# A causal convolution by matrices: its start rebuilt around an fp32 load of the history rows on SyncE's queue

## The chip, the cores and the metric

One core of a Trainium2 chip (trn2), as the page of the kernel before shows it: TensorE multiplies matrices (3620 matmuls) into tiles that the program keeps in PSUM (`pp` in the views); VectorE and ScalarE work element by element (764 and 460 instructions); loads are issued on GpSimd's queue (64 of x, 8 of the taps, 2 of the history), nearly all stores and the transposes of x on SyncE's (61 transposes); the page's DMA share is a mean over 16 DMA engines. The metric is the device time of one execution in microseconds (us); a run repeats it, and the medians below are of such runs. Experiments were timed on the same chip as the kernel before, in rounds with it. The first comparison was timed in six runs each, beforehand; the changed kernel was not timed again beside the experiments.

## The reference

```python
B, S, D, K = 8, 4096, 512, 8
out = 0
for k in range(K):
    shifted = x shifted down by k rows in S, zeros first      # k = 0: x itself
    out += matmul(shifted, kernel[k])                         # kernel[k] is 512 x 512
```

The sequence is cut into 128 runs of 256 rows, one run per partition (16 runs for each of the 8 batches). A run needs the last rows of the run ahead of it: its **history**. Partition p takes it from partition p-1's rows in memory; partition 0 has none, so a history load has 127 partitions. The first run of each batch (every sixteenth partition) must have zeros there.

## The kernel before

TensorE multiplies in bf16. The eight taps and the rows are combined in three levels of sums and differences (Karatsuba's trick; W holds 8 tap matrices and 19 differences), so that fewer products do. The main loop is steady; what the change touches is the start. There four history rows (H) and the first four rows (`xin[0, 0]`) are transposed and summed on TensorE by multiplying with the identity, `ident`; `identh` is the identity with zeros for the first runs. `direct` is one product of the first sixteen.

```python
def load(out, src):                      # casts fp32 to bf16 on the way
    nc.gpsimd.dma_start(out=out, in_=src)

H = D421
load(H[1:P, 4:8], xr[0:P - 1, RUN - 4:RUN, :])       # history, 127 partitions
load_x(0, 0)
ident = spool.tile([P, P], bf, name="ident")
make_identity(nc, ident)
identh = ...                             # cut: identh, identn, zero, by GpSimd and VectorE

def fill(pw):                            # warm-up: products that nobody reads
    for h in range(2):
        nc.tensor.matmul(pw[:, h], lhsT=ident, rhs=zero, start=True, stop=True)

for r in range(2):
    for k in range(4):
        fill(pair(k))                    # 16 matmuls
...
load_w(4)
transpose_pe("xh", 2, H, 5, 8)
sums_pe("d4a", 1, (-4, 0), (-3, 1))      # history row + x row, transposed, on TensorE
load(H[1:P, 1:4], xr[0:P - 1, RUN - 7:RUN - 4, :])
load_w(6)
sums_pe("d4b", 2, (-2, 2), (-1, 3))
...
direct(0, 2)                             # the first product
```

The first outputs of a node of the main loop go from PSUM into an "ms" buffer, of which there are two, and these also hold finished rows until their stores are done:

```python
mpool = ctx.enter_context(tc.tile_pool(name="m", bufs=2))
...
elif n.a == MID:
    ms[b_] = mpool.tile([P, 2, D], f32, name="ms")
    nc.scalar.copy(out=ms[b_], in_=p)
```

## Time and profile before

| | before |
|---|---|
| median time, 3 runs | 783.0 us (782.42 to 783.3) |
| span of the profiled execution | 780.9 us |
| TensorE busy | 767.4 us, 98% |
| VectorE busy | 659.3 us, 84% |
| history rows landed | 6.9 us |
| first product | 13.81 us |

An engine that is busy 98% of the span leaves only its few idle stretches to win or lose. The view of waits (who waited for whom: us in total, times, longest), cut to the first 100 us, shows those of TensorE after the warm-up; each is about one microsecond:

```profile
PE pp L192 <- DMA xin<-in_x_dram: 1.4, 1, 1.4
...
PE pp L192 <- ACT D L362: 1.1, 1, 1.1
PE pp L192 <- ACT XT L390: 1.1, 1, 1.1
...
PE pp L215 <- DVE pp L76: 0.9, 2, 0.7
PE pp L215 <- DMA w<-in_kernel_dram: 0.9, 1, 0.9
```

### The profile page before, as it was taken

To read this page: it belongs to the slowest core of one execution; us is meant where nothing else is said; L and a number is where in the kernel's file an instruction comes from. 1 tells how busy PE (TensorE), PEld (TensorE's weight loads), DVE (VectorE), ACT (ScalarE), POOL (GpSimd) and SP (SyncE) were. 2 spreads that over 40 slices of the span, in tenths; PEclk is the share of its full clock that TensorE was granted. 3 is DMA by queue.
4 is the path that set the end of the run, shared out by engine and by line. 5 is a ranking of instruction groups with operands and counts; after the bars stand their busy time and mean duration, and the time that the engine had idled before them with its cause. 6 is when DMAs were issued, how large, how long until landed. Compare 5 with 4: busy or idle time off the path is not lost.

```text
span 780.9 us, 9507 instructions
## 1 busy us (share of the span) xinstructions
PE 767.4 (98%) x3620; PEld 349.0 (45%) x3620; DVE 659.3 (84%) x764; ACT 283.2 (36%) x460; POOL 42.8 (5%) x83
## 2 busy tenths in 40 slices
PE   7899999999999999999999999999999999999997
PEld 4444444444444444444444444444444444444443
DVE  4899888888888889888898888898888898888895
ACT  2453433333333333343324343333343333343332
POOL 5000000000000000000000000000000000000000
PEclk9999999999999999999999999999999999999999
DMA  9963979778788777878777788877787877788753
GB/s 163 210 120 114 237 176 207 169 187 167 178 179 206 174 176 173 177 184 194 184 171 168 179 190 188 191 166 179 165 187 187 195 170 182 166 172 200 179 153 123
DMA packets 159229, 138.37 MB, mean 177 GB/s; under 512 B 130130, under 2 KB 134226, under 8 KB 159184
## 3 DMA queue, kind: packets, MB, share of 16 engines
q1 hardware_dynamic: 145312, 98.84, 46.3%
q0 software_dynamic: 13728, 38.66, 31.1%
q8 instruction: 28, 0.46, 0.2%
q10 hardware_dynamic: 144, 0.26, 0.1%
q14 instruction: 17, 0.14, 0.1%
HBM read 77.32 MB, written 67.11 MB: 185 GB/s over the span
## 4 chain that ended last, share of the span: by engine, by line
PE 94%; DMA 3%; DVE 1%; POOL 1%; issue 0%; ACT 0%; DVEq 0%; POOLq 0%
PE pp L215 94%; DMA xin<-in_x_dram 2%; DMA XT<-xin 1%; POOL w L80 0%; DVE D L76 0%; PE pp L192 0%; DVE pp L76 0%; ACT XT L390 0%; DVE y L76 0%; POOL D L80 0%; DVEq L648 0%; POOL xin L80 0%; POOL identn L148 0%; PE pp L186 0%; POOL ident masks.py:199 0%
## 5 line engine op out<-in xcount | busy, mean ns | idle before, releaser
L215 PE MATMUL pp<-w,D 128*128 128x512 bf16 x3280 | 715.8, 379 | 1.7 <-DMA w<-in_kernel_dram 0.9
L215 PEld LDWEIGHTS <-D 128*128 128x128 bf16 x3280 | 320.2, 98 | 390.4 <-issue 2.8
L76 DVE TENSOR_TENSOR D<-D 128x2048 bf16<-128x2048 bf16 (+2 forms) x250 | 227.2, 948 | 3.4 <-ACT D L369 3.4
L76 DVE TENSOR_TENSOR y<-pp,ms 128x1024 f32<-128x1024 f32 (+1 forms) x121 | 146.4, 1212 | 45.3 <-PE pp L215 45.3
L76 DVE TENSOR_TENSOR D<-XT 128x2048 bf16<-128x2048 bf16 (+2 forms) x153 | 142.5, 947 | 12.1 <-DMA XT<-xin 10.4
L262 ACT COPY pp<-pp 128x512 f32<-128x512 f32 x95 | 54.1, 570 | 260.6 <-PE pp L215 260.6
L274 ACT COPY pp<-pp 128x512 f32<-128x512 f32 x95 | 54.2, 570 | 167.1 <-PE pp L215 165.6
L76 DVE TENSOR_TENSOR pp<-dts,pp 128x512 f32<-128x512 f32 x95 | 65.7, 691 | 43.9 <-ACT dts L280 42.6
L317 ACT COPY ms<-pp 128x1024 f32<-128x1024 f32 x60 | 61.0, 1016 | 35.0 <-PE pp L215 33.0
L80 POOL DMA_DIRECT2D xin<-in_x_dram x64 | 34.0, 531 | 692.5 <-DMA XT<-xin 675.8
L290 DVE SCALAR_TENSOR_TENSOR pp<-pp,dts 128x512 f32<-128x512 f32 x95 | 66.0, 695 | 3.2
L280 ACT COPY dts<-pp 128x512 f32<-128x512 f32 x95 | 57.5, 606 | 0.0
L276 ACT ACTIVATE pp<-pp 128x512 f32<-128x512 f32 x95 | 56.1, 590 | 0.8 <-PE pp L215 0.8
L215 PE MATMUL pp<-w,XT 128*128 128x512 bf16 x120 | 30.8, 379 | 0.0
L76 DVE TENSOR_TENSOR w<-w,w 128x2048 bf16<-128x2048 bf16 x19 | 22.9, 1219 | 1.5 <-DMA w<-in_kernel_dram 1.3
L215 PEld LDWEIGHTS <-XT 128*128 128x128 bf16 x120 | 11.7, 98 | 14.2
L186 PE MATMUL pp<-zero,ident 128*128 128x512 bf16 x20 | 6.7, 493 | 3.1 <-POOL ident masks.py:199 3.1
L215 PE MATMUL pp<-w,F 128*128 128x512 bf16 x36 | 8.7, 379 | 0.2 <-DVE pp L76 0.2
L215 PE MATMUL pp<-w,w 128*128 128x512 bf16 x36 | 8.3, 379 | 0.0
L192 PE MATMUL pp<-ident,xin 128*128 128x128 bf16 x48 | 3.2, 219 | 3.6 <-DMA xin<-in_x_dram 1.4
L80 POOL DMA_DIRECT2D w<-in_kernel_dram x8 | 6.1, 785 | 0.5 <-DMA w<-in_kernel_dram 0.5
L358 DVE COPY D<-pp 128x1536 bf16<-128x1536 bf16 x1 | 1.0, 958 | 6.1 <-PE pp L192 6.1
(59 smaller groups left out, 78.7 us busy)
## 6 DMA issues: line engine op xcount, KB each, us to landing
out_dram<-y SPq DMA_DIRECT2D x123, 512.0 KB, 3.4
xin<-in_x_dram POOLq DMA_DIRECT2D x64, 512.0 KB, 6.0
w<-in_kernel_dram POOLq DMA_DIRECT2D x8, 512.0 KB, 15.7
out_dram<-ms SPq DMA_DIRECT2D x2, 512.0 KB, 5.4
out_dram<-f SPq DMA_DIRECT2D x2, 512.0 KB, 6.3
XT<-xin SPq DMA_TRANSPOSE x61, 6.1
D<-in_x_dram POOLq DMA_DIRECT2D x1, 508.0 KB, 5.6
D<-in_x_dram POOLq DMA_DIRECT2D x1, 381.0 KB, 9.4
```

What stands on the lines that cost most here:

```text
L76: nc.vector.tensor_tensor(out=o, in0=a, in1=b, op=op)
L80: nc.gpsimd.dma_start(out=out, in_=src)
L186: nc.tensor.matmul(pw[:, h], lhsT=ident, rhs=zero, start=True, stop=True)
L192: nc.tensor.transpose(o[:, t - t0, c * P:(c + 1) * P], src[:, t, c * P:(c + 1) * P], ident)
L215: nc.tensor.matmul(bank, lhsT=comp[:, c * P:(c + 1) * P], rhs=w[:, c, :], start=start and c == 0, stop=c == DC - 1, skip_group_check=True)
L262: nc.scalar.copy(out=n.q[:, 0], in_=n.q[:, 1])
L274: nc.scalar.copy(out=n.p[b_][:, 1], in_=n.q[:, 1])
L276: nc.scalar.mul(out=n.p[b_][:, 1], in_=n.q[:, 1], mul=-1.0)
L280: nc.scalar.copy(out=n.dts, in_=n.q[:, 0])
L290: nc.vector.scalar_tensor_tensor(out=p[:, 0], in0=p[:, 1], scalar=-1.0, in1=n.dts, op0=MUL, op1=SUB)
L317: nc.scalar.copy(out=ms[b_], in_=p)
L358: nc.vector.tensor_copy(out=XF[:, 0:3], in_=bank["xh"])
```

## The change

The intent: let the history load start first, on a queue of its own, and have GpSimd issue its casting loads before it builds the identity. The load on SyncE's queue does not cast here, so the rows land as fp32 in D421's space, and VectorE and ScalarE cast them. The sums move from TensorE to VectorE, which makes `identh` needless; the warm-up multiplies zeros by zeros, so that it need not wait for the identity, and has 12 matmuls instead of 16. The order of the start after that (some 200 lines) is another one.

```diff
-    H = D421
-    load(H[1:P, 4:8], xr[0:P - 1, RUN - 4:RUN, :])
+    H, HF = XT, D421.bitcast(f32).rearrange("p (t b) d -> p t (b d)", b=2)
+    nc.sync.dma_start(out=HF[1:P], in_=xr[0:P - 1, RUN - 4:RUN, :])
     load_x(0, 0)
-    ident = ...; make_identity(nc, ident); identh = ...; identn = ...
 ...
+    load_w(4)
+    load(H[1:P, 1:4], xr[0:P - 1, RUN - 7:RUN - 4, :])
+    ident = spool.tile([P, P], bf, name="ident")
+    make_identity(nc, ident)
 ...
-            nc.tensor.matmul(pw[:, h], lhsT=ident, rhs=zero, start=True, stop=True)
+            nc.tensor.matmul(pw[:, h], lhsT=zero[:, 0:P], rhs=zero, start=True, stop=True)
 ...
-    for r in range(2):
-        for k in range(4):
-            fill(pair(k))
+    for k in range(6):
+        fill(pair(k % 4))
 ...
-    transpose_pe("xh", 2, H, 5, 8)
-    sums_pe("d4a", 1, (-4, 0), (-3, 1))
+    nc.vector.tensor_copy(out=H[:, 4:6], in_=HF[:, 0:2])
+    nc.scalar.copy(out=H[:, 6:8], in_=HF[:, 2:4])
+    transpose_pe("h0", 3, H, 4, 6)
+    transpose_pe("h1", 0, H, 6, 8)
+    nc.scalar.copy(out=XF[:, 0:2], in_=bank["h0"])
+    transpose_pe("x0", 2, xin[0, 0], 0, 2)
+    nc.scalar.copy(out=XF[:, 4:6], in_=bank["x0"])
+    tt(D4[:, 0:2], XF[:, 0:2], XF[:, 4:6], ADD)          # the first sum, on VectorE
 ...                                                       (the rest is order)
```

More of the change, by code (lines that the diff above doesn't have):

```diff
@@ L136, in pair @@
         return ppool.tile([P, 2, D], f32, name=f"pp{k}")
-    H = D421
-    load(H[1:P, 4:8], xr[0:P - 1, RUN - 4:RUN, :])
+    H, HF = XT, D421.bitcast(f32).rearrange("p (t b) d -> p t (b d)", b=2)
+    nc.sync.dma_start(out=HF[1:P], in_=xr[0:P - 1, RUN - 4:RUN, :])
     load_x(0, 0)
-    ident = spool.tile([P, P], bf, name="ident")
-    make_identity(nc, ident)
-    identh = spool.tile([P, P], bf, name="identh")
-    nc.gpsimd.tensor_copy(out=identh, in_=ident)
-    nc.gpsimd.memset(identh[:, 0:P:G], 0.0)
-    identn = spool.tile([P, P], bf, name="identn")
-    nc.gpsimd.tensor_scalar_mul(out=identn, in0=ident, scalar1=-1.0)
     zero = spool.tile([P, D], bf, name="zero")
@@ L151 @@
     U1 = zero
-    nc.vector.memset(H[0:1], 0.0)
+    nc.vector.memset(HF[0:1], 0.0)
+    nc.vector.memset(H[0:1, 1:4], 0.0)
     def load_w(tap):
@@ L168, in mid_dve @@
         tt(o, u, v, SUB)
+    load_w(4)
+    load(H[1:P, 1:4], xr[0:P - 1, RUN - 7:RUN - 4, :])
+    ident = spool.tile([P, P], bf, name="ident")
+    make_identity(nc, ident)
     bank = {}
-    def mid_pe(h, k, *which):
-        o, u, v = mid(*which)
-        bank[which, h] = pair(k)
-        for c in range(2):
-            pw = bank[which, h][:, c]
-            nc.tensor.matmul(pw, lhsT=ident, rhs=u[:, 2 * h + c], start=True, stop=False)
-            nc.tensor.matmul(pw, lhsT=identn, rhs=v[:, 2 * h + c], start=False, stop=True)
-    def mid_act(h, *which):
-        nc.scalar.copy(out=mid(*which)[0][:, 2 * h:2 * h + 2], in_=bank[which, h])
     def fill(pw):
         for h in range(2):
-            nc.tensor.matmul(pw[:, h], lhsT=ident, rhs=zero, start=True, stop=True)
+            nc.tensor.matmul(pw[:, h], lhsT=zero[:, 0:P], rhs=zero, start=True, stop=True)
     def transpose_pe(name, k, src, t0, t1):
@@ L194, in transpose_pe @@
         bank[name] = o[:, 0:t1 - t0]
-    def sums_pe(name, k, *sums):
-        pw = bank[name] = pair(k)
-        for h, ts_ in enumerate(sums):
-            for c in range(DC):
-                for n, t in enumerate(ts_):
-                    src, idt = (xin[0, 0][:, t], ident) if t >= 0 else (H[:, 8 + t], identh)
-                    nc.tensor.matmul(pw[:, h, c * P:(c + 1) * P], lhsT=src[:, c * P:(c + 1) * P],
-                                     rhs=idt, start=n == 0, stop=n == len(ts_) - 1,
-                                     skip_group_check=True)
-    for r in range(2):
-        for k in range(4):
-            fill(pair(k))
+    for k in range(6):
+        fill(pair(k % 4))
     XF = D42
@@ L346, with first_run @@
     C0, C1 = W[MID, HI, MID], W[MID, LO, MID]
-    load_w(4)
-    transpose_pe("xh", 2, H, 5, 8)
-    sums_pe("d4a", 1, (-4, 0), (-3, 1))
-    load(H[1:P, 1:4], xr[0:P - 1, RUN - 7:RUN - 4, :])
-    load_w(6)
-    sums_pe("d4b", 2, (-2, 2), (-1, 3))
-    nc.vector.tensor_copy(out=XF[:, 0:3], in_=bank["xh"])
-    transpose_pe("xf", 2, xin[0, 0], 0, 4)
-    load_w(5)
-    nc.vector.tensor_copy(out=D4[:, 0:2], in_=bank["d4a"])
-    nc.scalar.copy(out=D4[:, 2:4], in_=bank["d4b"])
-    n0.p = {0: pair(0), 1: pair(1)}
+    def first_run(z):
+        nc.vector.memset(z[:, :, 0:D:G], 0.0)
@@ new lines @@
+    nc.vector.tensor_copy(out=H[:, 4:6], in_=HF[:, 0:2])
+    nc.scalar.copy(out=H[:, 6:8], in_=HF[:, 2:4])
+    n0.p = {0: pair(0), 1: pair(1)}
+    load_w(6)
+    transpose_pe("h0", 3, H, 4, 6)
+    transpose_pe("h1", 0, H, 6, 8)
+    nc.scalar.copy(out=XF[:, 0:2], in_=bank["h0"])
+    first_run(XF[:, 0:2])
+    transpose_pe("x0", 2, xin[0, 0], 0, 2)
+    nc.scalar.copy(out=XF[:, 4:6], in_=bank["x0"])
+    tt(D4[:, 0:2], XF[:, 0:2], XF[:, 4:6], ADD)
+    load_w(5)
+    transpose_pe("xb", 3, xin[0, 0], 2, 4)
@@ L364 @@
+    nc.scalar.copy(out=XF[:, 2:4], in_=bank["h1"])
+    direct(0, 0)
+    nc.vector.tensor_copy(out=XF[:, 6:8], in_=bank["xb"])
+    first_run(XF[:, 2:4])
     fill(pair(3))
+    transpose_pe("he", 1, H, 1, 4)
+    tt(D4[:, 2:4], XF[:, 2:4], XF[:, 6:8], ADD)
     load_w(7)
+    load_x(0, 1)
+    tt(D2, XF[:, 1:6], XF[:, 3:8], ADD)
     direct(0, 2)
+    direct(0, 3)
+    load_x(1, 0)
+    tt(E4[:, 1:4], bank["he"], XF[:, 1:4], ADD)
+    direct(2, 2)
     direct(0, 1)
-    direct(0, 3)
-    nc.scalar.copy(out=XF[:, 3:7], in_=bank["xf"])
@@ L370 @@
-    sums_pe("e4a", 2, (-5, -1), (-6, -2))
-    nc.vector.memset(XF[:, 0:3, 0:D:G], 0.0)
-    tt(D2, XF[:, 0:5], XF[:, 2:7], ADD)
-    direct(2, 3)
-    tt(F21, D2[:, 0:4], D2[:, 1:5], ADD)
-    mid_dve(1, LO, HI)
-    sums_pe("e4b", 2, (-7, -3))
-    direct(1, 2)
-    direct(0, 0)
-    load_x(0, 1)
-    tt(D1, XF[:, 2:4], XF[:, 3:5], ADD)
-    mid_dve(2, LO, HI)
-    nc.scalar.copy(out=E4[:, 3:1:-1], in_=bank["e4a"])
-    mid_dve(2, LO, LO)
-    load_x(1, 0)
-    load_w(0)
-    nc.vector.tensor_copy(out=E4[:, 1], in_=bank["e4b"][:, 0])
@@ L387 @@
-    direct(1, 3)
-    direct(1, 1)
-    transpose_pe("x1", 2, xin[0, 1], 0, 4)
-    nc.scalar.copy(out=XT[:, 4:8], in_=bank["x1"])
+    first_run(E4[:, 1:4])
+    direct(1, 1)
+    tt(D1, XF[:, 3:5], XF[:, 4:6], ADD)
+    mid_dve(1, LO, HI)
+    nc.vector.tensor_copy(out=F0, in_=XF[:, 4])
+    mid_dve(2, LO, HI)
+    tt(F21, D2[:, 0:4], D2[:, 1:5], ADD)
+    direct(2, 0)
+    mid_dve(2, LO, LO)
     load_w(2)
     mid_dve(1, LO, LO)
+    load_w(0)
+    direct(1, 3)
+    direct(2, 3)
+    mid_dve(2, LO, MID)
@@ L393 @@
     direct(1, 0)
-    transpose_pe("x2", 2, xin[1, 0], 0, 4)
-    mid_dve(2, LO, MID)
-    load_w(1)
-    tt(D4[:, 4:8], XF[:, 3:7], XT[:, 4:8], ADD)
-    direct(2, 1)
-    nc.vector.tensor_copy(out=XT[:, 2:4], in_=bank["x2"][:, 2:4])
+    transpose_pe("x1", 2, xin[0, 1], 0, 4)
+    nc.vector.tensor_copy(out=XT[:, 4:8], in_=bank["x1"])
+    tt(D4[:, 4:8], XF[:, 4:8], XT[:, 4:8], ADD)
+    direct(1, 2)
+    tt(D42[:, 3], D4[:, 1], D4[:, 3], ADD)
+    transpose_pe("x2", 2, xin[1, 0], 0, 4)
+    prep_d41(HI)
@@ L400 @@
+    direct(3, 2)
+    nc.scalar.copy(out=XT[:, 0:2], in_=bank["x2"][:, 0:2])
+    direct(3, 3)
+    nc.scalar.copy(out=XT[:, 2:4], in_=bank["x2"][:, 2:4])
+    nc.scalar.copy(out=C0[:, 0:2], in_=XT[:, 6:8])
+    nc.scalar.copy(out=C1, in_=XT[:, 0:4])
     prep_d42(HI)
-    nc.scalar.copy(out=XT[:, 0:2], in_=bank["x2"][:, 0:2])
-    nc.scalar.copy(out=C0[:, 0:2], in_=XT[:, 6:8])
     tt(T4, XT[:, 4:8], XT[:, 0:4], ADD)
+    direct(3, 0)
+    fill(pair(2))
     direct(3, 1)
-    prep_d41(HI)
-    tt(T42[:, 0:2], D4[:, 6:8], T4[:, 0:2], ADD)
@@ L407 @@
-    direct(3, 0)
-    nc.scalar.copy(out=C1, in_=XT[:, 0:4])
-    direct(2, 0)
-    nc.scalar.copy(out=F0, in_=XF[:, 3])
-    direct(3, 3)
-    fill(pair(2))
     tt(D41[:, 1], T4[:, 0], T4[:, 1], ADD)
     load_w(3)
+    node_a1(1)
+    direct(2, 1)
+    node_u(nodes[1])
+    tt(D41[:, 0], D4[:, 7], T4[:, 0], ADD)
+    tt(T42[:, 0:2], D4[:, 6:8], T4[:, 0:2], ADD)
+    tt(D421[:, 0], D42[:, 7], T42[:, 0], ADD)
     tt(T42[:, 2:4], T4[:, 0:2], T4[:, 2:4], ADD)
-    node_a1(1)
-    direct(2, 2)
+    mid_dve(1, HI, HI)
@@ L418 @@
+    load_w(1)
     node_e(nodes[0], 0)
-    tt(D41[:, 0], D4[:, 7], T4[:, 0], ADD)
+    load_x(1, 1)
+    load_x(2, 0)
+    prep_d27()
+    mid_dve(2, HI, LO)
     node_a0(nodes[1])
-    node_u(nodes[1])
-    direct(3, 2)
-    mid_dve(1, HI, HI)
     node_seed(nodes[1], 0)
-    prep_d27()
+    node_v(nodes[1], 0)
     node_dts(nodes[1])
+    tt(D421[:, 1:4], T42[:, 0:3], T42[:, 1:4], ADD)
+    node_d(nodes[1], 0)
     node_seed(nodes[1], 1)
-    tt(D42[:, 3], D4[:, 1], D4[:, 3], ADD)
-    node_v(nodes[1], 0)
@@ L430 @@
-    tt(D421[:, 0], D42[:, 7], T42[:, 0], ADD)
-    load_x(1, 1)
+    mid_dve(1, HI, LO)
+    node_e(nodes[0], 1)
+    mid_dve(2, HI, HI)
     node_v(nodes[1], 1)
-    tt(D421[:, 1:4], T42[:, 0:3], T42[:, 1:4], ADD)
+    mid_dve(2, HI, MID)
+    node_l(nodes[1], 0, HI)
+    load_x(2, 1)
+    node_d(nodes[1], 1)
+    prep_d421(HI)
+    mid_dve(0, HI, HI)
     node_a1(2)
-    mid_dve(2, HI, LO)
+    node_l(nodes[1], 0, LO)
+    node_e(nodes[1], 0)
     transpose_x(1, 1)
-    mid_dve(1, HI, LO)
-    node_d(nodes[1], 0)
@@ L439 @@
-    node_l(nodes[1], 0, LO)
-    mid_dve(2, HI, MID)
-    nc.scalar.copy(out=D4[:, 2:4], in_=T4[:, 2:4])
-    node_d(nodes[1], 1)
-    load_x(2, 1)
-    node_e(nodes[0], 1)
-    node_u(nodes[2])
-    node_l(nodes[1], 0, HI)
-    node_e(nodes[1], 0)
-    node_a0(nodes[2])
-    node_seed(nodes[2], 0)
-    prep_d421(HI)
-    load_x(2, 0)
-    mid_dve(2, HI, HI)
-    node_l(nodes[1], 1, LO)
-    node_l(nodes[1], 1, HI)
-    nc.scalar.copy(out=U1, in_=XT[:, 0])
-    node_v(nodes[2], 0)
-    prep_d4(HI)
@@ L458 @@
-    nc.scalar.copy(out=D42[:, 3], in_=T42[:, 3])
-    node_seed(nodes[2], 1)
-    node_v(nodes[2], 1)
-    node_dts(nodes[2])
-    mid_dve(0, HI, HI)
-    node_e(nodes[1], 1)
-    prep_d41(HI)
-    node_d(nodes[2], 0)
-    node_l(nodes[2], 0, HI)
-    tt(A1[:, 0], C0[:, 1], C1[:, 0], ADD)
-    prep_d42(HI)
-    node_d(nodes[2], 1)
-    transpose_x(2, 0)
-    mid_dve(0, LO, HI)
+    node_a0(nodes[2])
+    node_u(nodes[2])
+    node_l(nodes[1], 1, LO)
+    node_seed(nodes[2], 0)
+    prep_d4(HI)
@@ L472 @@
+    nc.scalar.copy(out=D4[:, 2:4], in_=T4[:, 2:4])
+    node_l(nodes[1], 1, HI)
+    node_seed(nodes[2], 1)
+    node_dts(nodes[2])
+    node_v(nodes[2], 0)
+    node_d(nodes[2], 0)
+    node_e(nodes[1], 1)
+    node_v(nodes[2], 1)
+    node_l(nodes[2], 0, HI)
+    nc.scalar.copy(out=D42[:, 3], in_=T42[:, 3])
+    prep_d41(HI)
+    mid_dve(0, LO, LO)
+    nc.scalar.copy(out=U1, in_=XT[:, 0])
     node_a1(3)
     node_l(nodes[2], 0, LO)
+    node_d(nodes[2], 1)
     node_a0(nodes[3])
     node_e(nodes[2], 0)
-    mid_dve(0, LO, LO)
+    prep_d42(HI)
@@ L477 @@
+    node_l(nodes[2], 1, LO)
+    node_u(nodes[3])
+    node_seed(nodes[3], 0)
+    node_l(nodes[2], 1, HI)
+    mid_dve(0, HI, LO)
+    node_seed(nodes[3], 1)
     tt(D421[:, 0:4], D42[:, 3:7], D42[:, 4:8], ADD)
-    node_u(nodes[3])
-    node_l(nodes[2], 1, HI)
-    node_seed(nodes[3], 1)
-    node_seed(nodes[3], 0)
+    node_e(nodes[2], 1)
     node_dts(nodes[3])
+    mid_dve(0, LO, HI)
+    node_v(nodes[3], 1)
+    tt(A1[:, 0], C0[:, 1], C1[:, 0], ADD)
     mid_dve(1, MID, HI)
-    node_v(nodes[3], 1)
+    node_v(nodes[3], 0)
@@ L485 @@
     node_d(nodes[3], 1)
-    mid_dve(0, HI, LO)
-    node_v(nodes[3], 0)
     node_d(nodes[3], 0)
-    node_l(nodes[2], 1, LO)
     node_a1(4)
+    node_l(nodes[3], 1, HI)
     mid_dve(1, MID, LO)
+    node_l(nodes[3], 0, LO)
+    node_a0(nodes[4])
+    node_l(nodes[3], 0, HI)
+    node_dts(nodes[4])
     tt(D21[:, 2:4], C1[:, 0:2], C1[:, 2:4], ADD)
-    node_l(nodes[3], 1, HI)
-    node_l(nodes[3], 0, LO)
     mid_dve(2, MID, MID)
-    node_e(nodes[2], 1)
+    tt(D21[:, 0:2], C0[:, 0:2], C1[:, 0:2], ADD)
@@ L497 @@
+    tt(A1[:, 1], C1[:, 0], C1[:, 1], ADD)
     load_x(3, 0)
-    node_l(nodes[3], 0, HI)
-    node_a0(nodes[4])
-    tt(D21[:, 0:2], C0[:, 0:2], C1[:, 0:2], ADD)
+    transpose_x(2, 0)
+    mid_dve(2, MID, LO)
+    node_e(nodes[3], 0)
     node_u(nodes[4])
-    node_e(nodes[3], 0)
+    node_seed(nodes[4], 0)
+    mid_dve(2, MID, HI)
     node_l(nodes[3], 1, LO)
-    tt(A1[:, 1], C1[:, 0], C1[:, 1], ADD)
-    mid_dve(2, MID, LO)
-    mid_dve(2, MID, HI)
-    node_seed(nodes[4], 0)
+    node_seed(nodes[4], 1)
@@ L508 @@
     node_v(nodes[4], 0)
-    node_seed(nodes[4], 1)
-    node_dts(nodes[4])
+    node_e(nodes[3], 1)
     node_d(nodes[4], 0)
@@ L513 @@
     node_v(nodes[4], 1)
-    prep_m()
     node_l(nodes[4], 0, HI)
     node_l(nodes[4], 0, LO)
+    node_u(nodes[5])
+    prep_m()
     node_a0(nodes[5])
-    node_e(nodes[3], 1)
+    node_seed(nodes[5], 0)
     node_d(nodes[4], 1)
-    node_u(nodes[5])
-    node_seed(nodes[5], 0)
+    node_y(nodes[4], 0, LO)
+    tt(F21[:, 0], D2[:, 0], D21[:, 0], ADD)
+    node_y(nodes[4], 0, HI)
     node_l(nodes[4], 1, LO)
-    tt(F21[:, 0], D2[:, 0], D21[:, 0], ADD)
+    prep_d4(LO)
     node_l(nodes[4], 1, HI)
-    node_y(nodes[4], 0, LO)
-    node_y(nodes[4], 0, HI)
-    store(0, LO, 0, first[0, LO, 0])
-    tt(F21[:, 1], D21[:, 0], D21[:, 1], ADD)
     node_dts(nodes[5])
     node_v(nodes[5], 0)
+    store(0, LO, 0, first[0, LO, 0])
+    node_seed(nodes[5], 1)
+    node_y(nodes[4], 1, LO)
     prep_d27()
-    node_seed(nodes[5], 1)
+    node_d(nodes[5], 0)
+    node_v(nodes[5], 1)
+    node_d(nodes[5], 1)
     store(0, HI, 0, first[0, HI, 0])
+    tt(F21[:, 1], D21[:, 0], D21[:, 1], ADD)
+    node_y(nodes[4], 1, HI)
+    node_a1(6)
+    node_l(nodes[5], 0, LO)
+    node_a0(nodes[6])
     load_x(3, 1)
-    node_y(nodes[4], 1, LO)
-    node_v(nodes[5], 1)
-    node_d(nodes[5], 0)
-    node_d(nodes[5], 1)
+    transpose_x(2, 1)
+    node_l(nodes[5], 0, HI)
+    store(0, LO, 1, first[0, LO, 1])
+    node_u(nodes[6])
     tt(F21[:, 2:4], D21[:, 1:3], D21[:, 2:4], ADD)
-    node_l(nodes[5], 0, LO)
-    node_l(nodes[5], 0, HI)
-    node_a1(6)
-    node_l(nodes[5], 1, HI)
-    node_u(nodes[6])
-    prep_d4(LO)
-    store(0, LO, 1, first[0, LO, 1])
-    node_y(nodes[4], 1, HI)
-    node_a0(nodes[6])
-    node_y(nodes[5], 0, LO)
-    prep_d41(LO)
-    transpose_x(2, 1)
-    node_l(nodes[5], 1, LO)
-    store(0, HI, 1, first[0, HI, 1])
-    node_seed(nodes[6], 0)
-    node_v(nodes[6], 0)
-    node_y(nodes[5], 0, HI)
+    prep_d41(LO)
+    node_y(nodes[5], 0, HI)
+    node_l(nodes[5], 1, LO)
+    node_seed(nodes[6], 0)
+    store(0, HI, 1, first[0, HI, 1])
+    node_y(nodes[5], 0, LO)
+    node_v(nodes[6], 0)
+    node_l(nodes[5], 1, HI)
+    store(1, LO, 0, first[1, LO, 0])
+    node_dts(nodes[6])
+    store(1, HI, 0, first[1, HI, 0])
     tt(D21[:, 0:2], D2[:, 0:2], D2[:, 1:3], ADD)
-    node_dts(nodes[6])
+    node_d(nodes[6], 0)
+    node_y(nodes[5], 1, HI)
+    node_y(nodes[5], 1, LO)
     node_seed(nodes[6], 1)
@@ L561 @@
     tt(D21[:, 2:4], D2[:, 2:4], D2[:, 3:5], ADD)
-    node_d(nodes[6], 0)
+    node_d(nodes[6], 1)
     prep_d42(LO)
-    node_y(nodes[5], 1, HI)
-    node_d(nodes[6], 1)
-    store(1, LO, 0, first[1, LO, 0])
-    node_y(nodes[5], 1, LO)
-    store(1, HI, 0, first[1, HI, 0])
+    store(1, HI, 1, first[1, HI, 1])
     node_a1(7)
-    store(1, HI, 1, first[1, HI, 1])
     prep_d4(HI)
```

## The prediction

> **What bounds the kernel now.** I read the page first (the shares of the engines, then the same in 40 slices), then the windows view for the start, then the timeline and the landings of the first loads. The page says which engine is the limit:
>
> ```profile
> PE 767.4 (98%) x3620; PEld 349.0 (45%) x3620; DVE 659.3 (84%) x764; ACT 283.2 (36%) x460; POOL 42.8 (5%) x83
> ...
> PE   7899999999999999999999999999999999999997
> ...
> L215 PE MATMUL pp<-w,D 128*128 128x512 bf16 x3280 | 715.8, 379 | 1.7 <-DMA w<-in_kernel_dram 0.9
> ```
>
> TensorE is busy in 98% of the span, and its products waited 1.7 us in all. So only the start and the tail can change the time. The windows view (columns: stretch and length; busy of PE, PEld, DVE, ACT, POOL with counts; clock; DMA share; GB/s) splits the span where the first product starts (13.8):
>
> ```profile
> 0.00:13.80 13.80, 9.51 (x78) 5.67 (x79) 4.36 (x5) 2.52 (x3) 6.97 (x17) 1.00 0.85 147
> 13.80:34.00 20.20, 16.57 (x116) 8.76 (x115) 15.78 (x17) 8.57 (x7) 4.62 (x7) 1.00 1.19 207
> 34.00:100.00 66.00, 64.99 (x297) 28.71 (x296) 62.83 (x76) 29.53 (x47) 2.11 (x4) 1.00 0.70 159
> 100.00:700.00 600.00, 600.00 (x2781) 271.48 (x2779) 511.40 (x594) 216.28 (x361) 27.48 (x52) 1.00 0.79 181
> ```
>
> TensorE lacks 3.6 us in 13.8 to 34, 1.0 in 34 to 100, nothing in 100 to 700. Before 13.8 it does only warm-up, transposes and sums. Its whole time is therefore: 13.8 us to the first product, then 767.1 us of nearly closed work up to 780.9. In the start the DMA engines are full (share 1.19, 207 GB/s from 13.8 to 34). The timeline (start, length, engine, line, operation, wait before) shows the four rows of history first in the queue, the warm-up and the first products:
>
> ```profile
> 1.23 0.68 POOL L80 DMA_DIRECT2D D<-in_x_dram  x1 [0.80 <-POOLq L637]
> ...
> 3.10 5.51 PE L186 MATMUL pp<-zero,ident 128*128 128x512 bf16 x16 [3.10 <-POOL ident masks.py:199]
> ...
> 13.81 2.75 PE L215 MATMUL pp<-w,D 128*128 128x512 bf16 x12
> ```
>
> and the page's DMA issues (KB each as written, median us from issue to landing) give its duration:
>
> ```profile
> D<-in_x_dram POOLq DMA_DIRECT2D x1, 508.0 KB, 5.6
> ```
>
> The history load (127 partitions of 4 rows, 508 KB as written in bf16) takes 5.6 us from issue to landing, so it is there at 6.9, before the 16 warm-up matmuls end.
>
> [...] (5.6 us for a 127-partition load cannot be one engine, see below). No run so far has a 127-partition load on SyncE's queue; its stores have 128 partitions.
> [...] warm-up matmuls start 0.43 us apart from 3.1 to 6.9, later ones run at about 0.216 us.
>
> **The change part by part.**
>
> *History load on SyncE's queue.* The rate of one DMA engine: software-queue loads move 38.66 MB by the page, while HBM was read for 77.32 MB, so a casting load reads twice what the GB/s column counts. 207 GB/s written over 16 engines is 207 x 2 / 16 = 26 GB/s read for each engine. Stores fit: a 512 KB store, 1.3 us at that rate, lands 3.4 us after issue, so some 2 us are fixed. The load now reads 127 x 8192 B = 1.04 MB. On all engines that is 2.5 us; on one it is 1.04 MB / 26 GB/s = **40 us**. That engine also has its sixteenth of the casting loads queued meanwhile: x rows, four taps, three history rows, x rows; 6.75 loads of 1 MB, at 2.5 us each (1.05 MB / (26 x 16) GB/s), so 17 us. If both queues are served in turn, the casting loads end first and the history needs 40 + 17 = 57 us of this engine; if the short packets of the taps (2 KB read) get less of it, some 52. With 2 us to the first packet and the receipt, I choose landing at **58.5 us**, instead of 6.9.
>
> *After the landing.* The casts of the rows (VectorE two, ScalarE two) come first in their engines' order, and TensorE's first transposes wait for them, so nothing useful passes by. Chain: cast of 128x1024, 1.0 (ScalarE's 128x1024 copies take 1.01 to 1.05); [...] ScalarE's copy of them 1.0 and of the x transposes 1.0; VectorE's sum of 128x1024, 0.7; hand-overs 0.3: 5.2 us. First product at 58.5 + 5.2 = 63.7.
>
> *After the first product.* The same products follow, 767.1 us before. The waits of the old start for DMA mostly go: 3.6 us lacking in 13.8 to 34, as the four taps and two blocks of x have landed by then. The next x block is issued when the x transposes have freed its buffer (4.6 us after the landing) and needs 5.1 as a lone load does here at 45.6; the last four taps follow 2.5 us apart, up to 20 us after the landing, ahead of the node that needs them (22 products of 0.86 us after the first). After the first product 44 small transposes at 0.055 us stand in place of 56 transposes and sums: 0.7 less. [...] VectorE is busy 62.8 of 66 us in 34 to 100 and gets about 3.5 us more work (two sums, a longer E4 sum, larger copies, two clearings): I put half of it, 1.7, on the path. Sum: 767.1 - 3.6 - 0.7 + 1.0 + 1.7 = 765.5.
>
> *The rest.* Identity later and its two variants gone: GpSimd's, off the path. Warm-up on zeros: starts at about 1.1 instead of 3.1, four matmuls fewer; worth nothing if the data come at 58. The steady state and tail are unchanged.
>
> Span 63.7 + 765.5 = 829.2; the reported time lies 2.1 above the span (783.0 against 780.9): **831 us**, 6.1% longer.
>
> **Rivals.**
> (a) *The load is spread over 16 engines.* For it: the author's intent, and that GpSimd's 127-partition load is spread. Then it lands near 7 to 8 us beside the x rows, the chain of 5.2 gives a first product at about 12, some 2 us earlier; but the 12.75 MB of the start still need 12.75 x 2.5 = 32 us of full DMA, so later waits move little: 778 to 785, same. [...]
> (b) *One engine, but with a greater share or faster.* If SyncE's queue is served first, landing near 44 to 49: 816 to 822. Served last or with slower 8 KB rows: up to 65, 838.
> (c) *VectorE becomes the limit of the start.* All of its first 60 us of work now follows the landing, with no idle to work ahead (it had 3.4 and 1.3 us waits before). If all its added 3.5 us and some order conflicts count: 834 to 838. If (a) holds, it makes 785 to 788 and eats the gain.
>
> **Range and chances.** One engine: I give it 88%; (a) has 12%. Within one engine the landing has the spread 48 to 63, and the rest plus or minus 3. Time 831, range 817 to 840. The 2% border is at 798.7: slower 0.87; same 0.12; faster 0.01.
>
> **What would show it.** The page's DMA issues: the history load on SP with 45 to 60 us to landing (about 5 to 7 would be rival a). The 40 slices: TensorE empty from about 6 to near 60. The chain that ended last: some 7% on the DMA of the history rows. The DMA share falls to about a sixteenth between the end of the queued loads and the landing. TensorE's first product within 4 to 7 us of the landing and nearly no gaps after 70. The prediction is wrong if the load is spread, if TensorE finds other work ahead of it, or if VectorE's waits after the landing add up to over 5 us.

With them went the ground for one engine, so that the 88% stand as the author's estimate, and two terms of the sums: 1.2 us for eight transposes, in a chain that came to 5.2 us, and 1.0 us for a restart of TensorE at half clock, in a sum after the first product that came to 767.1 - 3.6 - 0.7 + 1.0 + 1.7 = 765.5. The 63.7, 829.2 and 831 us contain both. What was measured of them stands below, under "Why the prediction was right".

## The result, and the profile after

| | before | after |
|---|---|---|
| median time, 6 runs each | 783.28 us | 835.73 us (835.38 to 837.62) |
| span of the profiled execution | 780.9 us | 833.5 us |
| history rows landed | 6.9 us | 56.95 us |
| first product | 13.81 us | 63.25 us |
| first product to end | 767.1 us | 770.25 us |

The ratio is 1.0677 (95% interval 1.0663 to 1.069). Ratios here are the mean time of one kernel's fast runs over that of the other's of the same rounds, so not quite the ratio of the medians quoted.

The page of the changed kernel, in its parts: engines, the 40 slices, and the DMA issues (KB, us to landing).

```profile
PE 768.4 (92%) x3576; PEld 348.5 (42%) x3576; DVE 661.6 (79%) x770; ACT 281.8 (34%) x460; POOL 41.2 (5%) x79
...
PE   2018998999999999999999999999999999999997
...
DMA  9009448677787778887777787787778778778753
...
D<-in_x_dram SPq DMA_DIRECT2D x1, 1016.0 KB
```

TensorE does the same work (768.4 against 767.4 us) in a longer span: the second and third slice, 21 to 62 us, are empty or nearly so. The DMA engines are nearly empty then too: something is slow, but the memory is not busy. The issue row gives no landing for the history load (nor do those of e2_two); it is read from who waited for it. The waits of the first 125 us:

```profile
ACT L333 <- DMA D<-in_x_dram: 57.0, 1, 57.0
DVE XT L332 <- DMA D<-in_x_dram: 52.9, 1, 52.9
...
PE pp L180 <- DVE XT L332: 51.2, 1, 51.2
```

Two engines wait for one transfer, and TensorE waits for one of them. The windows view says how fast that transfer ran (last two columns: DMA share and GB/s):

```profile
4.00:20.00 16.00, 2.50 (x6) 0.60 (x4) 0.07 (x1) 0.00 (x0) 2.54 (x4) 0.70 1.16 209
22.00:56.00 34.00, 0.00 (x0) 0.00 (x0) 0.00 (x0) 0.00 (x0) 0.00 (x0) 0.50 0.07 23
```

A DMA share of 0.07 is one engine of sixteen (0.0625) and a little more; 23 GB/s is a ninth of what the sixteen write at 4 to 20. The timeline from the landing to the first product:

```profile
56.95 1.28 ACT L333 ACT_TABLE_LOAD   x1 [56.95 <-DMA D<-in_x_dram]
56.98 0.69 DVE L332 CAST XT<-D 128x1024 bf16<-128x1024 f32 x1 [52.91 <-DMA D<-in_x_dram]
...
58.25 1.04 ACT L333 CAST XT<-D 128x1024 bf16<-128x1024 f32 x1
59.20 1.00 ACT L338 COPY D<-pp 128x1024 bf16<-128x1024 bf16 x1
...
61.27 1.01 ACT L341 COPY D<-pp 128x1024 bf16<-128x1024 bf16 x1 [1.07 <-PE pp L180]
...
63.25 1.02 PE L191 MATMUL pp<-w,D 128*128 128x512 bf16 x4 [1.29 <-ACT D L345]
```

It is the chain that was foreseen, with one link more: ScalarE's first instruction is now behind the wait, and its table load of 1.28 us with it. In the kernel before that load ran at 0.72 us, where it cost nothing.

One loss stands far from the start. The timeline at 125 to 137 us:

```profile
125.46 0.53 POOL L80 DMA_DIRECT2D xin<-in_x_dram  x1 [21.96 <-DMA XT<-xin]
...
126.77 0.33 SPq L276 DMA_DIRECT2D out_dram<-ms  x1
...
134.82 1.01 ACT L293 COPY ms<-pp 128x1024 f32<-128x1024 f32 x1 [4.87 <-DMA out_dram<-ms]
...
136.38 1.06 PE L191 MATMUL pp<-w,D 128*128 128x512 bf16 x3 [2.77 <-ACT pp L250]
```

ScalarE waited 4.87 us for a store of an ms buffer to be done, and TensorE 2.77 us for ScalarE. The store took some 8 us from issue (126.77); the kernel before has the same store at 77.96, ahead of its x load, and no such wait of TensorE:

```profile
77.96 0.44 SPq L300 DMA_DIRECT2D out_dram<-ms  x1
...
79.78 0.53 POOL L80 DMA_DIRECT2D xin<-in_x_dram  x1 [23.66 <-DMA XT<-xin]
```

The experiments come back to this order. In the windows 136 to 138 and 138 to 140 the granted clock (TensorE's speed as a share of the full one) is 0.70 and 0.50: the pause also cost TensorE its clock for a while.

### The profile page after: what moved, and what is told of

Its sections match the earlier page's. It is cut to its first block, busy times and chain, and to the rows that moved or that the text cites. A ratio compares the mean times of both kernels' runs of the same rounds, so it can differ in the third digit from the quotient of the medians.

```text
span 833.5 us, 9433 instructions
## 1 busy us (share of the span) xinstructions
PE 768.4 (92%) x3576; PEld 348.5 (42%) x3576; DVE 661.6 (79%) x770; ACT 281.8 (34%) x460; POOL 41.2 (5%) x79
## 3 DMA queue, kind: packets, MB, share of 16 engines
q0 software_dynamic: 13584, 38.14, 29.4%
HBM read 77.32 MB, written 67.11 MB: 173 GB/s over the span
## 4 chain that ended last, share of the span: by engine, by line
PE 82%; DVE 7%; another core or an unknown queue 7%; DMA 2%; issue 1%; ACT 1%; DVEq 0%; SPq 0%; ACTq 0%
PE pp L191 82%; DVE D L76 3%; DVE w L76 2%; DVE y L76 1%; DMA out_dram<-ms 1%; DMA XT<-xin 1%; DVE pp L266 0%; DVE pp L76 0%; PE pp L180 0%; ACT pp L250 0%; ACT L333 0%; DVE F L76 0%; DVE XT L378 0%; DVE ms L76 0%
## 5 line engine op out<-in xcount | busy, mean ns | idle before, releaser
L76 DVE TENSOR_TENSOR D<-D 128x1024 bf16<-128x1024 bf16 (+1 forms) x252 | 228.4, 946 | 1.9 <-ACT D L341 1.7
L76 DVE TENSOR_TENSOR y<-pp,ms 128x1024 f32<-128x1024 f32 (+1 forms) x121 | 146.5, 1211 | 47.2 <-PE pp L191 47.2
L293 ACT COPY ms<-pp 128x1024 f32<-128x1024 f32 x60 | 61.0, 1016 | 36.8 <-PE pp L191 31.9
L180 PE MATMUL pp<-ident,XT 128*128 128x128 bf16 x28 | 2.9, 271 | 51.8 <-DVE XT L332 51.2
L180 PEld LDWEIGHTS <-XT 128*128 128x128 bf16 x28 | 2.3, 122 | 53.2 <-DVE XT L332 52.1
L191 PEld LDWEIGHTS <-XT 128*128 128x128 bf16 x120 | 11.7, 98 | 14.2
```

The lines of the kernel that those rows point to most:

```text
L76: nc.vector.tensor_tensor(out=o, in0=a, in1=b, op=op)
L180: nc.tensor.transpose(o[:, t - t0, c * P:(c + 1) * P], src[:, t, c * P:(c + 1) * P], ident)
L191: nc.tensor.matmul(bank, lhsT=comp[:, c * P:(c + 1) * P], rhs=w[:, c, :], start=start and c == 0, stop=c == DC - 1, skip_group_check=True)
```

## The experiments

Two theories stood at the beginning. **One engine**: SyncE's queue puts a load of 127 partitions on one DMA engine, so 1.04 MB take 50 us instead of 3. **The rest of the change**: fp32 rows, casts on chip, sums on VectorE and the new order cost the time, or fp32 rows 512 KB apart are slow to read whoever asks. Eleven kernels were run, all correct; the times of the kernel before beside them are 783.6 us.

| run | edit on | median us | ratio to before (95%) | history landed | first product |
|---|---|---|---|---|---|
| e1_spread | after | 788.56 | 1.0059 (1.0046 to 1.0072) | 7.6 | 13.86 |
| e2_two | after | 811.15 | 1.0351 (1.0332 to 1.037) | 32.5 | |
| e3_gpsimd | after | 789.05 | 1.0063 (1.0049 to 1.0076) | 8.6 | |
| e4_before_sync | before | 833.65 | 1.0638 (1.0619 to 1.0657) | 57 | 67.70 |
| e5_act | after | 836.40 | 1.0674 (1.0661 to 1.0688) | 57.0 | 62.51 |
| e6_ms | after | 831.64 | 1.0613 (1.0599 to 1.0627) | 57 | |
| e7_spread_ms | after | 782.67 | 0.9991 (0.9979 to 1.0003) | 7.5 | 13.72 |
| e10_spread_warm | after | 781.16 | 0.9977 (0.9964 to 0.999) | 7.3 | 12.78 |
| e11_all | after | 780.87 | 0.9965 (0.9952 to 0.9977) | 7.4 | 11.94 |
| e12_rows | after | 843.28 | 1.0761 (1.0739 to 1.0783) | 63.1 | 69.36 |
| e13_act_warm | after | 834.24 | 1.0648 (1.0632 to 1.0665) | 57 | 61.40 |

### e1_spread: the same load, same queue, in two parts

```diff
-    nc.sync.dma_start(out=HF[1:P], in_=xr[0:P - 1, RUN - 4:RUN, :])
+    nc.sync.dma_start(out=HF[1:113], in_=xr[0:112, RUN - 4:RUN, :])
+    nc.sync.dma_start(out=HF[113:P], in_=xr[112:P - 1, RUN - 4:RUN, :])
```

> The changed kernel with the history load cut in two on the same SyncE queue: 112 partitions [...] and 15 partitions. Theory (the 127-row load sits on one DMA engine): both parts land within 10 us of the start instead of 56.9, first product at 11 to 14 us, time 781 to 791 (835.7 less some 49 us of later landing, with DMA waits of the start coming back). Rival (the reordered start, the fp32 buffer and the casts on chip cost the time): stays over 820.

Measured: 788.56 us. Both parts landed by 7.6 us; the page's DMA issues:

```profile
D<-in_x_dram SPq DMA_DIRECT2D x1, 896.0 KB, 6.0
...
D<-in_x_dram SPq DMA_DIRECT2D x1, 120.0 KB, 6.3
```

How many engines each part had was not read; 896 KB in 6.0 us are 153 GB/s, by an estimate six engines' worth or so at the 26 GB/s of one (e12_rows below). Two lines in place of one take 47.2 of the 52.4 us away. The bytes, the queue, the fp32 buffer and the casts are what they were, so none of those is the main cost. The remaining 5 us, with a first product at 13.86 as early as before (13.81), are a second question.

### e2_two: a dose between

122 and 5 partitions, in the expectation that the larger part is spread over two engines.

```diff
-    nc.sync.dma_start(out=HF[1:P], in_=xr[0:P - 1, RUN - 4:RUN, :])
+    nc.sync.dma_start(out=HF[1:123], in_=xr[0:122, RUN - 4:RUN, :])
+    nc.sync.dma_start(out=HF[123:P], in_=xr[122:P - 1, RUN - 4:RUN, :])
```

> The changed kernel with the load cut into 122 partitions [...] and 5. Theory: 61 rows per engine at the 0.43 us per row that the changed kernel showed (54.9 us for 127), so landing at about 29 us and a time of about 808 (803 to 813), half way between one engine and sixteen. Rival (a fixed cost of this queue or of casts): 835 or, if cutting in two alone helps, as with 112 and 15.

Measured: 811.15 us, landing at 32.5. The share of busy DMA engines while only this load runs doubles, and so does its rate:

```profile
24.00:31.00 7.00, 0.00 (x0) 0.00 (x0) 0.00 (x0) 0.00 (x0) 0.00 (x0) 0.50 0.13 43
```

0.13 is two of sixteen engines (0.125). The landing was 3.5 us later than expected, the time within the expected range. Landing at 7.6, 32.5 and 57 us gives 788.6, 811.2 and 835.7: from 32.5 to 57 the time follows one for one, and below that nearly so. Nothing useful goes past this transfer.

### e3_gpsimd: the same fp32 load, issued by GpSimd

```diff
-    nc.sync.dma_start(out=HF[1:P], in_=xr[0:P - 1, RUN - 4:RUN, :])
+    nc.gpsimd.dma_start(out=HF[1:P], in_=xr[0:P - 1, RUN - 4:RUN, :])
```

> The changed kernel with the same fp32 load of 127 partitions issued by GpSimd instead of SyncE, nothing else changed. Theory (the queue's way of spreading 127 partitions): lands within 10 us, time 781 to 791. Rival (fp32 rows of 8 KB at a pitch of 512 KB are slow to read on any queue): over 820.

Measured: 789.05 us, with 7.4 us from issue to landing, in one piece with all 127 partitions. So fp32 rows of 8 KB, 512 KB apart, are read about as fast as e1_spread's two parts (6.0 and 6.3 us); it is the queue that makes the difference for 127 partitions: 7.4 us here, and a landing at 56.95 on SyncE's. A queue of its own was not worth much: 0.5 us separates this run from e1_spread, less than their spread.

### e4_before_sync: this part alone, in the kernel before

```diff
-    load(H[1:P, 4:8], xr[0:P - 1, RUN - 4:RUN, :])
+    HF = XT.bitcast(f32).rearrange("p (t b) d -> p t (b d)", b=2)
+    nc.sync.dma_start(out=HF[1:P], in_=xr[0:P - 1, RUN - 4:RUN, :])
 ...
+    nc.vector.tensor_copy(out=H[:, 4:6], in_=HF[:, 0:2])
+    nc.scalar.copy(out=H[:, 6:8], in_=HF[:, 2:4])
```

> The kernel before with this one part of the change alone: the four history rows loaded as fp32 on SyncE's queue into the idle XT buffer and cast by VectorE and ScalarE; order, sums and warm-up as before. Theory: landing at about 57 us, time 822 to 835. Rival (the reordered start is what costs): 783 to 787.

Measured: 833.65 us. The old order with this one load is within 2.1 us of the whole change. Together with e1_spread and e3_gpsimd the main question is settled: it is the load, both when taken out and when put in alone.

### e12_rows: who gets how much of the shared engine

The prediction had the casting loads end first, as both queues would be served in turn. In the changed kernel they did not: the first tap landed at 25.8, the last casting load at 61.8, five us after the history. In the trace the history's packets are 8192 bytes, the taps' packets 1024 bytes as written, so 2 KB as read (the page has 38.14 MB written by the casting loads' queue, and HBM read for 77.32 MB). Four loads of one row each make the history's packets 2 KB too.

```diff
-    nc.sync.dma_start(out=HF[1:P], in_=xr[0:P - 1, RUN - 4:RUN, :])
+    for t in range(4):
+        nc.sync.dma_start(out=HF[1:P, t], in_=xr[0:P - 1, RUN - 4 + t, :])
```

> The changed kernel with the history load issued as four loads of one row each: still 127 partitions, one engine, but packets of 2 KB instead of 8 KB. Theory (an engine serves its two queues one packet each in turn): the taps' packets read 2 KB too, so the taps get half of the engine instead of a fifth; the first tap lands near 16 instead of 25.8, all casting loads by 42 instead of 61.8, and the history last, near 60; time 836 to 840. Rival (shares are by time or bytes, whatever the packets): first tap still near 25, history near 57, 835.7. Counter-result for the one-engine theory: landing under 30.

Measured: the first tap landed at 15.5 us (13.6 after its issue, against 23.9 in the changed kernel), the last casting load at 37.9 and the history at 63.1. The view of the first tap in the changed kernel, then in this one:

```profile
DMA to landing us min/median/max: 23.9/23.9/23.9
...
DMA to landing us min/median/max: 13.6/13.6/13.6
```

That fits packets taken turn and turn about. The list of packets in the trace of the changed kernel shows it directly: from 22 to 56 us exactly one packet of the casting loads lies between any two of the history's (83 times of 83); with a tap's packet such a pair takes about 0.4 us, 0.32 of it the history's, so about four fifths. The time, 843.28 us, was above the expected 836 to 840, as the history landed 3 us later than I had reckoned. The reckoning was too low: the engine shared by both queues was done with them at 61.8 us in the changed kernel already. While the history has its engine alone (39 to 59 us of this run) the rate is 26 GB/s, so it is not the short packets that are slow. The landing and the time move together, by 6.1 and 7.6 us against the changed kernel. The other 1.5 us were not followed up; in this run's profile TensorE was at half clock until about 78 us, nine us past the first product, and in the changed kernel's it was not.

### e6_ms: the stall at 134 us

```diff
-            ms[b_] = mpool.tile([P, 2, D], f32, name="ms")
+            ms[b_] = (F21.bitcast(f32).rearrange("p (t b) d -> p t (b d)", b=2)
+                      if n.k == 6 and b_ == LO else mpool.tile([P, 2, D], f32, name="ms"))
```

> The changed kernel, with the first output buffer of the first node of the main loop taken from F21 (idle by then) instead of a buffer whose store is still under way. Theory: the wait of ScalarE of 4.87 us for that store cost TensorE 2.77 us of idle time and then some 1.7 us at half clock, so the time falls by 3.5 to 5, to about 831. Rival: TensorE would be held there by something else (VectorE, the next store) and the time stays within 1 us of 835.7.

Measured: 831.64 us, 4.1 less. ScalarE's copy no longer waits for a store, and TensorE runs through. Timeline of this kernel:

```profile
127.48 12.89 PE L191 MATMUL pp<-w,D 128*128 128x512 bf16 x59
...
131.13 1.01 ACT L294 COPY F<-pp 128x1024 f32<-128x1024 f32 x1 [1.10 <-PE pp L191]
```

### e5_act: the table load off the path

```diff
+    warm = spool.tile([1, 16], bf, name="warm")
+    nc.scalar.copy(out=warm, in_=zero[0:1, 0:16])
     nc.vector.tensor_copy(out=H[:, 4:6], in_=HF[:, 0:2])
```

> The changed kernel with a tiny ScalarE copy first, so that its table load (1.28 us, now behind the wait for the history rows) is done while they are still on their way. Theory: on the path from landing to first product, which shortens by 0.8 to 1.3, time about 834.6. Rival: VectorE's cast sets the first transposes and the table load is hidden: no change. Nearly the size of the noise; the trace (landing to first product, 6.3 us so far) decides.

Measured: 836.40 us, no gain, though the first product came at 62.51 instead of 63.25. In its profile the clock was at 0.50 from 57 to 64, and the first products ran at half speed; in the profile of the changed kernel it was at full speed from 62 on (the changed kernel, then this one; the clock is the column before the last two):

```profile
62.00:64.00 2.00, 0.75 (x4) 0.48 (x5) 1.49 (x4) 1.20 (x2) 1.74 (x3) 1.00 0.44 31
...
57.00:64.00 7.00, 5.08 (x36) 4.00 (x37) 3.02 (x7) 3.98 (x4) 2.35 (x4) 0.50 0.20 21
```

So the 0.7 us were won and lost again. The runs agree: of the changed kernel's six, four with a mean clock of 0.964 to 0.967 took 835.4 to 835.8 us and two with 0.963 took 837.3 and 837.6; the four of this run are all at 0.963 and took 836.0 to 837.2. That the clock is why is tested by the next run.

### e13_act_warm: both, kept warm

As e5_act, with 248 warm-up matmuls instead of 12, which last until the rows land.

```diff
-    for k in range(6):
+    for k in range(124):
```

> The changed kernel with the table loaded first and warm-up matmuls up to the landing (248 instead of 12). Theory: e5_act showed 0.7 us gained up to the first product and lost again because its clock stayed at half until about 66; kept warm, the time is 833 to 835. Rival: no gain from either (835.5 to 836.5), the path after the first product decides.

Measured: 834.24 us, 2.2 less than e5_act and 1.5 less than the changed kernel, first product at 61.40. The clock is full where e5_act's was half:

```profile
57.00:64.00 7.00, 4.78 (x52) 3.31 (x52) 4.14 (x7) 3.89 (x4) 3.52 (x5) 1.00 0.36 61
```

The 2.2 us against e5_act are the warm clock's. The 1.5 us against the changed kernel are less sure: the two intervals just touch (1.0632 to 1.0665, and 1.0663 to 1.069).

### e7_spread_ms: the early load without the stall

e1_spread with the edit of e6_ms:

```diff
+            ms[b_] = (F21.bitcast(f32)...  if n.k == 6 and b_ == LO else mpool.tile(...))
```

> The load cut into 112 and 15 partitions, and the first node's buffer from F21 as in e6_ms. Theory: 788.6 less the same 3.5 to 5, about 784.3, level with the kernel before. Rival: with the early start the stall belongs to the burst of stores and moves to the next buffer: 787 to 789.

Measured: 782.67 us, level with the kernel before, but its six runs lie from 781.4 to 784.5. Their mean clocks go the same way, from 0.996 in the fastest to 0.990 in the two slowest. The profile is of the fastest: there TensorE was idle for 2.0 us at 6 to 8 us, and its clock was half for about 3.4 us only (an estimate from the mean of 0.88 over 0 to 14 us; the four products at 13.72 took 1.02 us, where e1_spread's at half clock took 1.87). What the clock did in the slower runs was not traced.

### e10_spread_warm: the early load, kept warm

e1_spread with 24 warm-up matmuls:

```diff
-    for k in range(6):
+    for k in range(12):
```

> The load cut into 112 and 15 partitions, and 24 warm-up matmuls instead of 12, so that TensorE works from 1.2 to some 8.3 us. Theory: the changed kernel's warm-up ends at 6.05, TensorE is idle for 2.3 us, and its clock is at half until about 20 us (0.79 over 14 to 34), which costs 2 to 4 us; kept warm, the time is 785 to 787. Rival: the start is paced by transfers and VectorE, and a warm clock gains nothing: 788 to 789.

Measured: 781.16 us, 7.4 less than e1_spread, more than the 2 to 4 that I expected. First the clock (the column before the last two), windows of e1_spread:

```profile
8.00:12.00 4.00, 2.66 (x28) 2.49 (x29) 0.40 (x2) 2.92 (x4) 0.00 (x0) 0.61 1.17 206
...
14.00:16.00 2.00, 2.00 (x5) 0.65 (x5) 1.80 (x4) 0.00 (x0) 1.78 (x3) 0.50 1.24 206
...
20.00:22.00 2.00, 2.00 (x6) 0.75 (x5) 2.00 (x3) 0.00 (x0) 0.00 (x0) 0.50 1.14 223
22.00:24.00 2.00, 2.00 (x10) 0.81 (x9) 2.00 (x3) 0.00 (x0) 0.00 (x0) 0.86 1.06 213
```

and of e10_spread_warm:

```profile
0.00:14.00 14.00, 11.19 (x62) 5.38 (x63) 5.50 (x9) 5.27 (x5) 7.78 (x17) 1.00 0.98 199
14.00:34.00 20.00, 17.77 (x115) 9.11 (x113) 18.74 (x24) 5.55 (x6) 2.27 (x4) 1.00 1.20 208
```

In e1_spread the warm-up ended at 6.05, TensorE was idle until 8.35, and the clock went to half and stayed there until about 22 us. At a clock of 0.50 a busy TensorE has six matmuls in 2 us (20 to 22), at 0.86 ten (22 to 24). With the longer warm-up the clock does not fall in the start (the 1.00 of the first window leaves out the first ten or so warm-up matmuls, which start 0.43 us apart, at half speed: the trace's clock record begins only when they are through), the first product comes 1.1 us earlier, and the twenty products behind it start at 16.46 instead of 18.91 and take 4.48 instead of 6.26 us.

Most of the rest of the 7.4 is the stall of e6_ms, which was in e1_spread (2.73 us of TensorE) and is not in this run, without its edit:

```profile
76.68 0.33 SPq L277 DMA_DIRECT2D out_dram<-ms  x1
...
77.11 0.53 POOL L80 DMA_DIRECT2D xin<-in_x_dram  x1 [23.20 <-DMA XT<-xin]
...
80.97 1.01 ACT L294 COPY ms<-pp 128x1024 f32<-128x1024 f32 x1 [1.10 <-PE pp L192]
```

Here the ms store is issued 0.4 us before the x load and takes 3.7 us; in the changed kernel the x load (125.46) is issued 1.3 us ahead of the store (126.77), and in e1_spread 1.3 us too, and the store takes 8. The kernel before has the order of this run (store at 77.96, load at 79.78). The other traces agree: in all nine of the changed kernel and its variants in which the x load is ahead, by 1.3 us each time, the ms stores take 7.9 to 9.1 us; where the first ms store is ahead (the kernel before, this run, e11_all) it takes 3.6 to 3.7. One of the nine is e13_act_warm, so a warm clock alone does not put the order right. So the new order of the start lets an x load of 1 MB slip in ahead of a store that a buffer waits for, or not, depending on a microsecond or two. This reading rests on the order in these traces; no run changed that order alone.

### e11_all: all four

The edits of e1_spread, e6_ms, e5_act and e10_spread_warm together:

```diff
+    nc.sync.dma_start(out=HF[1:113], in_=xr[0:112, RUN - 4:RUN, :])
+    nc.sync.dma_start(out=HF[113:P], in_=xr[112:P - 1, RUN - 4:RUN, :])
...
+    for k in range(12):
...
+            ms[b_] = (F21.bitcast(f32)...  if n.k == 6 and b_ == LO else mpool.tile(...))
...
+    nc.scalar.copy(out=warm, in_=zero[0:1, 0:16])
```

> The changed kernel with all four mends: load cut into 112 and 15 partitions, 24 warm-up matmuls, ScalarE's table loaded first, first main-loop buffer from F21. Theory: the terms that e10 did not have yet are the table load (0.7 us on the path from landing to first product in e5_act) and a stall that e10 already escaped, so 780 to 781, below the kernel before by 0.3 to 0.5%. Rival: the start is bounded by transfers and VectorE after the first products, so no gain over e10_spread_warm (781.2).

Measured: 780.87 us, from 780.52 to 781.14 in six runs; 0.35% below the kernel before (0.9965, interval up to 0.9977), clear of noise though within the 2% that counts as the same. It beats both kernels. Against e10_spread_warm the first product is 0.8 us earlier (11.94) but the median only 0.3: in this run TensorE waits up to 0.8 us for the x rows and VectorE 0.5 for a tap, so parts of the start now wait for transfers.

## Why the prediction was right

The range was 817 to 840 with 831 in it; 835.73 was measured. By its steps:

- **One engine.** Right, and the deciding step. No trace before the change had a load of 127 partitions on SyncE's queue, so the 88% were the author's estimate. In the changed kernel the DMA share is 0.07 from 22 to 56 us, about one of sixteen, and in the trace's list the load's packets follow one another, overlapping by 0.014 us at most. GpSimd's loads of the four rows, on 127 partitions too, were not held back so (5.6 us in the kernel before, 7.4 in e3_gpsimd). e1_spread, e2_two, e3_gpsimd and e4_before_sync show it from four sides. Rival (a), a load spread over all engines, would have been e1_spread's 788.6, above the 778 to 785 given for it, for want of a warm clock and because of the stall.
- **Landing at 58.5.** Measured 56.95; it was issued at 0.74, and its packets run from 1.70 to 56.5 us in the trace's list. The sum of 40 us for the history and some 17 for the casting loads on the same engine was about right. The order was not: with turns by packet, of which the history's (8192 bytes) are four times the taps' as read, the history ended first and the casting loads five microseconds later (61.8), as e12_rows explains. The prediction's remark that the short packets might get less pointed there, but "the casting loads end first" was its main case.
- **Chain of 5.2 us to the first product.** Measured 6.30. The eight transposes (1.2) took 1.04 us, at a clock of 0.50. The link that was missing is the table load of 1.28 us, which moved behind the wait with ScalarE's first instruction. The chain in the profile before shows it at 0.72 us; I did not ask what comes ahead of the first copy.
- **767.1 to 765.5 us after the first product.** Measured 770.25, 4.7 more: the mis-sized term. The part about waits for DMA in the start held: apart from the stall, TensorE lacks about 3 us from 63 to 130, in place of 4.6 from 13.8 to 100 before. What was missing is the stall behind the ms store, 4.1 us by e6_ms (4.5 by the two profiled spans). The sentence "The steady state and tail are unchanged" is the step that failed; the boundary between the start and the main loop is where stores, loads and transposes of the start pile up, and I had not looked at the order in which they are issued.
- **Restart at half clock, 1.0 more.** In the profiled execution the clock record has 0.50 from 10.50 to 61.70 us. TensorE resumed at 57.73, so its clock was full again 4.0 us later, before the first product (63.25), and this term was near nothing there; in e5_act's it was paid (0.50 from 57 to 64). e13_act_warm, without it and with the table load early, is 1.5 us faster than the change.
- **VectorE, 1.7.** Not measured by itself. VectorE's busy time grew by 2.3 us (661.6 against 659.3), not by 3.5. The chain of waits from 76 to 126 us is mostly VectorE's work, as rival (c) had it, yet TensorE lacks only 1.6 us there (busy 48.42 of 50).

The terms balance: landing 1.5 less, chain 1.1 more, rest 4.7 more, in all 4.3 us; the span is 833.5 against 829.2 predicted. Within the rest, the stall is about as large as the whole error, and the 1.0 for the clock was not paid; the remaining difference of about 1 us is not accounted for.

The parts meant to gain did gain something: with the load spread, the stall gone, the clock warm and the table early, the new start is 2.8 us faster than the old one by the medians. Which part of the new start gives this was not separated. One line hid it under 50 us.

## What to carry to other kernels

Before moving a load to SyncE's queue (ScalarE's was not tried here), look at the number of partitions, and try it in parts. Here 127 ran on one engine (DMA share 0.07, landing at 56.95 us), 122 and 5 on two (0.13, 32.5), and 112 and 15 landed at 7.6; the last was worth 47 us. That the engines go by the divisors of the number of partitions fits the two shares that were read (127 is prime, 122 is twice 61); it was not tested further. When a start is rebuilt, ask of each engine what its first instruction is now waiting for (a table load may be in front of it: 1.28 us, at 56.95 in the changed kernel, and at 0.74 in e5_act with a tiny copy first), whether the warm-up lasts until the data come, and whether the stores of the start still meet the loads in the same order. A DMA share near one sixteenth in a windows view while everything waits was the sign of a transfer on one engine here.

A short pause of TensorE was already a risk. Idle stretches of 2.0 us (e7_spread_ms), 2.3 us (e1_spread) and 2.77 us (the changed kernel, before 136.38) were followed by half clock; one of 1.56 us (e10_spread_warm, before 16.46) was not. In the changed kernel the clock record has the half clock from 136.79, 0.41 us after TensorE had resumed, to 140.20, so 3.41 us long; in e7_spread_ms it lasted about 3.4 us by the estimate above, and in e1_spread until about 22 us.
